# x's fourth form is spread over the first pair's products, its second form is split one product sooner, and a weight row is split ahead of h

## The chip, the cores and the metric

The kernel runs on one core of a Trainium2 chip. The metric is the device time of one execution in microseconds (us); lower is better. The engines are TensorE (PE, with PEld for its weight loads), VectorE (DVE), ScalarE (ACT), GpSimd (POOL) and SyncE (SP). SP, ACT and POOL can issue DMAs. Each engine works through its own instructions in the order in which the program wrote them, and waits for others by semaphores.

## The reference

One sequence of 512 frames with 1024 features runs through two layers. Each layer is FFN, mixer, FFN, and a gated per-layer input embedding (PLE); after each, `x = layer_norm(2 ** 0.5 * x + sublayer)`.

```python
def swiglu_ffn(x, w_gu, w_d):            # w_gu: 1024 x 5632, w_d: 2816 x 1024
    g, u = jnp.split(x @ w_gu, 2, axis=-1)
    return (jax.nn.silu(g) * u) @ w_d

for i in range(2):
    x = layer_norm(ALPHA * x + 0.5 * swiglu_ffn(x, ffn1_wgu[i], ffn1_wd[i]), ...)
    mix = mlstm_mixer(x, ...) if i == 0 else gmlp_mixer(x, ...)
    x = layer_norm(ALPHA * x + mix, ...)
    x = layer_norm(ALPHA * x + 0.5 * swiglu_ffn(x, ffn2_wgu[i], ffn2_wd[i]), ...)
    x = layer_norm(ALPHA * x + sigmoid(x @ ple_wg[i] + ple_bg[i]) * (p[i] @ ple_wp[i]), ...)
```

All of it is float32. The change touches the four FFNs and the first products of the mLSTM mixer that follows the first FFN.

## The kernel before, in words

**Numbers in two parts.** A float32 operand is split into a high part (an ACT copy to a shorter format, `hi`) and a low part (`lo = src - hi`). A product of two operands is then three matmuls (`mm3`, L394 to L398): high by high, high by low, low by high. The split of a weight tile is in `Weights.fill`: the high part on ACT at L281, the low part either on DVE (L290, or L296 when it is put off) or, for tiles in `by_dma`, by an ACT copy of the negated source (L287) and a DMA issued by POOL that accumulates the source onto it (L288).

**The queue of weights.** `Weights` holds a written-out order of tiles (`order`), each with a kind of buffer (`main`: 4 buffers, `rows`, `rowsx`, `extra`, ...). `take` hands the next split tile to a product; `release` gives a buffer back and calls `fill`, which splits the next tiles in order as long as buffers are free, the load is there, and `limit` (an index in `order`) isn't reached. While `apart` is set, low parts on DVE are not issued with the high part but put into `pending`; `lows(n)` issues the first n of them, and `take` issues those that its tile needs. While `apart` is set, `fill` also stops at a tile whose load was issued less than two products ago, as long as others are ready. When a low part is issued, its raw buffer counts as read and the next load is issued on SP.

**An FFN.** The 22 blocks of 128 hidden columns are done in chunks of 2, 4, 4, 4, 4, 4 (`FFN_CHUNKS`). The first four blocks are plain: chunk 0, and the first two of chunk 1. A plain step is one projection (`project`, gate or up, 24 matmuls of 512 columns), numbered (c, i) by chunk and step, i = 0 to 3. From then on the blocks come in pairs, and a pair's gate and up halves are computed with 7 products instead of 8 (`UpPair.product(r)`, r = 0 to 6, 24 matmuls of 256 columns each), with sums of weight blocks (`up_forms`) and sums of blocks of x (`UpForms`). The way down is done likewise for a chunk at a time, 7 group products (`Group`), which are put between the products of the next chunk: one behind each plain step, and one behind every second product of a pair. The last chunk has a plain way down (`down`), four rows of `wd` for four 128-frame blocks.

**x's forms.** `UpForms` makes four sums of blocks of x once per FFN: t1 to t4, in high and low parts. Its float32 work tiles are `x_a` (a), `x_f` twice (b and c) and `x_d` (d, for t4). The steps in `self.steps` are taken by `formed.step()` in the plain products, one each, and two each in the products (1, 2) and (1, 3): so t1 is made in (1, 1), the splits of t1 and t2 in (1, 2), and `x21` and `t4` (four DVE steps) in (1, 3). t2's split is two ACT copies and one accumulating DMA from POOL (L1047 to L1049). What is in `self.last` comes behind a product of the first pair: t3's split behind product 0, t4's high part (ACT, L1068) behind product 1, its low part (DVE, L1073) behind product 2. t4's high part goes to the tile of b, which t3's split reads; t4's low part to the tile of c. Product 2 uses t2, product 3 t1, product 4 t3, and product 6 t4.

**Behind a product of a pair** (`up_products`), in this order: the additions of the last group product to x (`group.add`), `pair.take(r)`, the group form's low part, `W.lows()`, the step of `formed.last`, `W.release()` with its splits, the silu (`pair.gate`), weight sums ahead of time (`form_ahead`); then, behind every second one, a group product, another release and a group form. `pair.take(r)` copies a PSUM bank out on ACT for r = 0, 2, 3 (L1111) and adds one on DVE for r = 1, 5 (L1114) and 4 (L1116). Products 0, 2, 4 and 6 write the same bank, products 3 and 5 another: product 4 can start when `take(2)` has read its bank.

**The last way down.** In an FFN ahead of a PLE stage, its four `wd` rows have the kinds `rowsx`, `main`, `rows`, `main`. `W.limit` stops `fill` ahead of the fourth until the products of the last chunk, and the splits of the last h, are issued.

**mLSTM's start.** `up_staged` makes the first three products of the mixer with 256 frames first, while the last blocks of x are turned (hooks), then the other 256.

Of the kernel before, what the change touches and what calls it, by code (L numbers as in the profile page):

```python
# [50 lines left out]
class Weights:  # L51
# [4 lines left out]
    def __init__(self, nc, raw_pool, split_pool):  # L56
        self.nc = nc
        self.pools, self.free = {"main": split_pool}, {"main": W_BUFS, "none": 0}
        self.raw_pools, self.raw_bufs = {"raw": raw_pool}, {"raw": RAW_BUFS}
        self.raw_free, self.raw_at, self.raw_tags = deque(range(RAW_BUFS)), {}, {}  # L60
        self.loads, self.left, self.raws = [], [], {}
        self.queues, self.held_raws = defaultdict(deque), defaultdict(deque)
        self.order, self.next_split, self.in_place, self.by_dma = [], 0, set(), set()
        self.ready, self.taken, self.held = deque(), deque(), []
        self.apart, self.pending, self.made, self.after, self.formed = False, deque(), {}, {}, set()
        self.boxes, self.rank, self.loaded_at, self.clock = [], {}, {}, 0
        self.limit, self.ahead, self.forced, self.sums = None, False, False, set()

    def open(self, kind, pool, n):
        self.pools[kind], self.free[kind] = pool, n  # L70
# [180 lines left out]
    def fill(self, most=1000, low=None, meanwhile=None):  # L251

        while most and self.next_split < len(self.order) and self.next_split != self.limit:
            kind, js, make = self.order[self.next_split]
            if not self.free.get(kind):
                return meanwhile
            for j in js or ():
                while j not in self.raws:
                    if not self.load(self.loads[j][1]):
                        return meanwhile  # L260
                if self.apart and self.ready and self.loaded_at[j] > self.clock - 2:
                    return meanwhile
            if self.ahead and not self.forced and make in self.sums and make not in self.made:
                return meanwhile
            shape = [P, 2, 512]
            if js is not None:
                while any(m not in self.formed for m in self.after.get(make, ())):
                    self.lows(1)
                src, used = self.made.pop(make, None) or make()
                shape = list(src.shape)  # L270
            hi = self.pools[kind].tile(shape, F32R, name="whi", tag="whi")
            lo = self.pools[kind].tile(shape, F32R, name="wlo", tag="wlo")
            self.free[kind] -= 1
            self.next_split += 1
            if js is None:
                make(hi, lo)
                continue
            parts = 2 if self.next_split == 1 else 1
            for i in range(parts):
                s = slice(i * shape[1] // parts, (i + 1) * shape[1] // parts)  # L280
                self.nc.scalar.activation(hi[:, s], src[:, s], AF.Copy)  # L281
                if meanwhile and make in self.in_place:
                    meanwhile()
                    meanwhile = None
                if make in self.by_dma or low == "dma" and make not in self.in_place:

                    self.nc.scalar.activation(lo[:, s], src[:, s], AF.Copy, scale=-1.0)  # L287
                    self.nc.gpsimd.dma_start(lo[:, s], src[:, s], accum_op=OP.add)  # L288
                elif not self.apart:
                    self.nc.vector.tensor_sub(lo[:, s], src[:, s], hi[:, s].bitcast(F32))  # L290
            self.ready.append((kind, (hi, lo)))
            most -= 1

            def done(make=make, used=used, src=src, hi=hi, lo=lo, late=self.apart and make not in self.by_dma):
                if late:
                    self.nc.vector.tensor_sub(lo, src, hi.bitcast(F32))  # L296
                self.formed.add(make)
                for j in used:
                    self.left[j] -= 1
                while self.load():  # L300
                    pass

            if self.apart and make not in self.by_dma:
                self.pending.append((lo, done))
            else:
                done()
        return meanwhile
# [58 lines left out]
def hybrid_trunk(ctx: ExitStack, tc, x, p, ln_g, ln_b, ffn1_wgu, ffn1_wd, ffn2_wgu, ffn2_wd,  # L366
# [125 lines left out]
    def ffn_weights(wgu, wd, name, ple=False):  # L492
        starts = [sum(FFN_CHUNKS[:c]) for c in range(LAST + 1)]

        def forms(c):
            m = FFN_CHUNKS[c] // 2

            def quarter(i, j):
                k = starts[c] + m * i
                return kp(wd)[:, k:k + m, j * 512:(j + 1) * 512]  # L500
            loads = [W.add_load(quarter(i, j), n, name) for i, j, n in ((0, 0, 2), (0, 1, 1), (1, 1, 1), (1, 0, 2))]
            return W.forms("rows", *((j, slice(None)) for j in loads))

        first = len(W.order)
        for at in range(PLAIN):
            if at == 0 or at == PLAIN - 1:
                W.add(*((kp(wgu)[:, :, c0:c0 + P], [slice(None)]) for c0 in (at * P, HID + at * P)))
            elif at % 2:
                add_pairs(wgu, at * P, HID + at * P)
        tiles = W.order[first:]  # L510
        del W.order[first:]
        for c, n in enumerate(FFN_CHUNKS):
            down_w = deque(forms(c - 1) if c else ())
            plain = plain_blocks(c)
            for i in range(2 * plain):
                W.order.append(tiles[2 * starts[c] + i])
                if down_w:
                    W.order.append(down_w.popleft())
            if plain < n:
                products = []  # L520
                for b in range(starts[c] + plain, starts[c] + n, 2):
                    products += W.up_forms(*(W.add_load(kp(wgu)[:, k:k + 4, c0:c0 + 2 * P], 1, "box")
                                             for c0 in (b * P, HID + b * P) for k in (0, 4)),
                                            by_dma=UP_BY_DMA if b == starts[c] + plain else UP_BY_DMA_2 if c < LAST else UP_BY_DMA_LAST)
                for s, product in enumerate(products):
                    W.order.append(product)
                    if down_after(c, s):
                        W.order.append(down_w.popleft())
        if ple:
            W.add_hook("rows", lambda hi, lo: turn_p.pop()(hi, lo))  # L530
        add_rows(wd, starts[LAST], 4, ["rowsx", "main", "rows", "main"] if ple else ["main", "rows", "rowsx", "rows"])
        ffn_ends.append(len(W.order) - (1 if ple else 0))


    ML_SLOTS = (2, 3, 4, 5, 6, 7, 11)
# [343 lines left out]
    def up_staged(first=False):  # L879
# [14 lines left out]
        for i, ps in enumerate(banks):  # L894
            w = W.take()
            ws.append(w)
            if i:
                up(ps, w, 0, 256, (((0,), (2, 7)) if first else ((), (0, 3)))[i - 1])
                continue
            if not first:  # L900
                run_hook()
            low_last(w, ps, 0, 256)
        low_last(ws[0], banks[0], 256, SEQ)
        for ps, w in zip(banks[1:], ws[1:]):
            up(ps, w, 256, SEQ)
        return banks

    def up_tokens(t, ws, ps, c=slice(0, 512), hook=None, release=None):
# [99 lines left out]
    class UpForms:  # L1008


        def __init__(self, pool, late):
# [33 lines left out]
            def split_t2():  # L1045
# [4 lines left out]

            self.steps = [
                x22, lambda: joined(b, 0, 1), t3, lambda: joined(c, 0, 0), lambda: vec.tensor_add(c, b, c),
                t1, split_t1, split_t2]

            d = [tmp.tile([P, 2, 256], F32, name="x_d", tag="pad", bufs=3) for _ in range(2)]

# [15 lines left out]
                for i, s in enumerate(halves):  # L1072
                    vec.tensor_sub(lo[:, s], d[i], self.t4[0][:, s].bitcast(F32))  # L1073

            self.steps += [x21, t4]
            self.last = {0: lambda: split(*self.t3, b), 1: t4_high, 2: t4_low}
            self.right = [self.quarter(0, 0), self.quarter(1, 0), self.t2, self.t1, self.t3,
                          self.quarter(1, 1), self.t4]

# [55 lines left out]
    def ffn(layer, k, rows, late, prepare=None):  # L1135
        with stage_pool("forms", 2) as fpool, stage_pool("quarters", Q_BUFS) as qpool, \
# [58 lines left out]
            for c, n in enumerate(FFN_CHUNKS):  # L1195
# [5 lines left out]
                if c == 0:  # L1201
                    formed = UpForms(tpool, late)
                W.apart, W.ahead = not plain, c > 0
                if c == LAST:
                    W.limit = ffn_ends.pop(0)
                for i in range(2 * plain):
# [16 lines left out]
                    if (c, i) in AFFINE_AT:  # L1223
                        run_affine(by_dma=True)
                    W.form_ahead(3)
                    for _ in range(1 if (c, i) < (1, 2) else 2):
                        formed.step()
                if c == 0:
                    group = Group(h, fpool, True)
                    group.form()  # L1230
                    group.form()
                else:
                    W.apart = True
                    next_group = up_products(c, n, h if c < LAST else None, plain)
                    if c < LAST:
                        next_group.form()
# [1 line left out]
                    group = next_group  # L1238
            W.limit = None
            W.fill()  # L1240
            W.apart = W.ahead = False
            return down(hs, False, norm, lazy=layer == 0, defer=prepare is not None)

    def ffn_stage(layer, k):
# [725 lines left out]
```

## Time and profile before

| what | us |
|---|---|
| median of 3 runs | 2197.59 (2197.32 to 2198.0) |
| the profiled execution | 2193.58 |
| its span, first to last instruction | 2191.9 |
| PE busy in the span | 2167.9 |
| DVE busy | 1761.8 |
| ACT busy | 1245.3 |

The mean granted clock of TensorE in the span is 0.996. A row of the timeline gives the start, the length, engine, line, operation and tiles (out<-in), and in brackets how long the engine had been idle before it and what ended that. A row of the list of waits gives who waited for whom: us in total, times, the longest. A row of the windows gives the stretch, its length, then the busy time of PE, PEld, DVE, ACT and POOL with the number of instructions, the granted clock, the DMA engines' busy share, and GB/s.

### The profile page before, as it was taken

The numbers are of one execution on the slowest core, as the hardware profiler recorded it, in microseconds if no ns is written. First come the engines' busy times: TensorE is split into PE (matmuls) and PEld (weight loads), VectorE is DVE, ScalarE is ACT, GpSimd is POOL, SyncE is SP. The second block draws the span as 40 slices with busy tenths as digits, with TensorE's granted clock in tenths as the row PEclk, the third lists the DMA queues.
The fourth block names the chain that finished last, engine by engine and source line by source line (L and its number), as shares of the span: only waits on it lengthen the run. The fifth ranks groups of instructions, "written<-read, shape, count | busy, mean of one in ns | idle before, by whom it ended". The sixth has DMA issues, their size and how long they took to land. (4 is left out here: it accounts for less than half of the span.)

```text
span 2191.9 us, 33268 instructions
## 1 busy us (share of the span) xinstructions
PE 2167.9 (99%) x13109; PEld 1934.6 (88%) x13109; DVE 1761.8 (80%) x2540; ACT 1245.3 (57%) x1712; POOL 253.8 (12%) x311
## 2 busy tenths in 40 slices
PE   9999999999999999999999999999999999999998
PEld 8899998888888889999888899998888888999987
DVE  6888887777776788888887888887788678888887
ACT  4766656464646456666445766655345455666642
POOL 1111101011101111111000111100011101111100
PEclk9999999999999999999999999999999999999999
DMA  7878764366847468787444887763338748877651
GB/s 218 195 185 192 175 166 124 78 156 134 165 112 155 124 156 206 187 202 167 144 132 131 199 194 185 177 158 125 132 77 155 163 125 202 193 189 177 137 170 58
DMA packets 232836, 346.28 MB, mean 158 GB/s; under 512 B 9780, under 2 KB 164532, under 8 KB 232680
## 3 DMA queue, kind: packets, MB, share of 16 engines
q0 software_dynamic: 56832, 117.64, 31.6%
q1 hardware_dynamic: 169232, 211.83, 29.8%
q10 hardware_dynamic: 6616, 14.69, 2.0%
q8 instruction: 103, 1.69, 0.3%
q14 instruction: 53, 0.43, 0.1%
HBM read 224.58 MB, written 2.11 MB: 103 GB/s over the span
## 5 line engine op out<-in xcount | busy, mean ns | idle before, releaser
L281 ACT ACTIVATE whi<-wbox 128x1024 fp32r<-128x1024 f32 x252 | 265.1, 1054 | 233.2 <-DVE wbox L144 99.9
L396 PE MATMUL ups<-xh,whi 128*128 128x256 f32 x1152 | 328.3, 285 | 7.8 <-ACT us L1111 7.8
L398 PE MATMUL ups<-xh,wlo 128*128 128x256 f32 x1152 | 328.1, 285 | 0.7 <-DMA wlo<-wbox 0.6
L397 PE MATMUL ups<-xl,whi 128*128 128x256 f32 x1152 | 327.9, 285 | 0.0
L396 PE MATMUL gps<-whi,fhi 128*128 128x512 f32 x644 | 253.0, 393 | 0.1
L281 ACT ACTIVATE whi<-wraw 128x1024 fp32r<-128x1024 f32 (+1 forms) x196 | 200.5, 1045 | 92.0 <-DVE wraw L121 22.6
L397 PE MATMUL gps<-wlo,fhi 128*128 128x512 f32 x644 | 252.3, 392 | 0.0
L398 PE MATMUL gps<-whi,flo 128*128 128x512 f32 x644 | 251.5, 391 | 0.0
L288 POOL DMA_DIRECT2D wlo<-wbox x160 | 135.6, 848 | 920.7 <-ACT wlo L287 502.9
L396 PEld LDWEIGHTS ups<-xh,whi 128*128 128x128 f32 x1152 | 222.8, 193 | 11.9 <-ACT us L1111 9.5
L397 PEld LDWEIGHTS ups<-xl,whi 128*128 128x128 f32 x1152 | 222.9, 194 | 2.4
L398 PEld LDWEIGHTS ups<-xh,wlo 128*128 128x128 f32 x1152 | 222.8, 193 | 1.1 <-DMA wlo<-wbox 1.1
L784 DVE TENSOR_TENSOR xt<-xt,gps 128x512 f32<-128x512 f32 x302 | 195.5, 681 | 29.1 <-PE gps L398 29.1
L290 DVE TENSOR_TENSOR wlo<-wraw,whi 128x1024 fp32r<-128x1024 f32 (+1 forms) x124 | 148.1, 1213 | 39.7 <-ACT whi L281 38.9
L281 ACT ACTIVATE whi<-wquarter 128x1024 fp32r<-128x1024 f32 (+1 forms) x140 | 135.2, 966 | 59.2 <-ACT wlo L287 20.4
L287 ACT ACTIVATE wlo<-wbox 128x1024 fp32r<-128x1024 f32 x160 | 167.1, 1044 | 0.0
L398 PEld LDWEIGHTS gps<-whi,flo 128*128 128x128 f32 x644 | 120.9, 188 | 26.9
L396 PEld LDWEIGHTS gps<-whi,fhi 128*128 128x128 f32 x644 | 121.3, 188 | 22.3 <-issue 0.2
L397 PEld LDWEIGHTS gps<-wlo,fhi 128*128 128x128 f32 x644 | 121.4, 188 | 21.3
L296 DVE TENSOR_TENSOR wlo<-wquarter,whi 128x1024 fp32r<-128x1024 f32 (+1 forms) x116 | 139.2, 1200 | 0.0
L966 DVE TENSOR_TENSOR flo<-h,fhi 128x512 fp32r<-128x512 f32 (+1 forms) x140 | 88.7, 636 | 53.5 <-ACT fhi L963 53.4
L963 ACT ACTIVATE fhi<-h 128x512 fp32r<-128x512 f32 (+1 forms) x140 | 80.3, 574 | 52.3 <-DVE h L1216 28.7
(367 smaller groups left out, 5806.8 us busy)
## 6 DMA issues: line engine op xcount, KB each, us to landing
wlo<-wbox POOLq DMA_DIRECT2D x160, 512.0 KB, 5.8
wbox<-in_ffn_wgu_dram SPq DMA_DIRECT2D x144, 512.0 KB, 4.6
wquarter<-in_ffn_wd_dram SPq DMA_DIRECT2D x64, 512.0 KB, 6.1
wraw<-in_ml_w_in_dram SPq DMA_DIRECT2D x24, 1024.0 KB, 5.8
wlo<-wraw POOLq DMA_DIRECT2D x48, 512.0 KB, 6.5
wraw<-in_gm_w_in_dram SPq DMA_DIRECT2D x15, 1024.0 KB, 5.8
wraw<-in_ffn_wgu_dram SPq DMA_DIRECT2D x17, 512.0 KB, 5.5
wraw<-in_ffn_wd_dram SPq DMA_DIRECT2D x8, 1024.0 KB, 4.9
```

Of the source, the lines that this page charges most:

```text
L281: self.nc.scalar.activation(hi[:, s], src[:, s], AF.Copy)
L287: self.nc.scalar.activation(lo[:, s], src[:, s], AF.Copy, scale=-1.0)
L288: self.nc.gpsimd.dma_start(lo[:, s], src[:, s], accum_op=OP.add)
L290: self.nc.vector.tensor_sub(lo[:, s], src[:, s], hi[:, s].bitcast(F32))
L296: self.nc.vector.tensor_sub(lo, src, hi.bitcast(F32))
L396: mm(ps, st[0], mv[0], start=start, stop=False, skip_group_check=more)
L397: mm(ps, st[0], mv[1], start=False, stop=False, skip_group_check=more)
L398: mm(ps, st[1], mv[0], start=False, stop=stop, skip_group_check=more)
L784: vec.tensor_add(dst, dst, ps)
L963: sca.activation(hi, src, AF.Copy)
L966: vec.tensor_sub(lo, src, hi.bitcast(F32))
```

## The change

- x's forms: `split_t2` is taken in (1, 1), `t1` in (1, 2), `split_t1` in (1, 3), one step per plain product. `x21` and `t4` come behind products 1 and 2 of the first pair, `t4_high` and `t4_low` behind products 3 and 4.
- The limit in an FFN ahead of a PLE stage lies behind the fourth row of `wd` instead of ahead of it.
- A new flag `hold` takes over the second meaning of `apart` (stopping at a fresh load). Behind the first FFN `apart` stays set through its way down and into `up_staged` of the mLSTM mixer, `hold` doesn't; `up_staged` issues the pending low parts one at a time between its products and then clears `apart`.

```diff
-                if self.apart and self.ready and self.loaded_at[j] > self.clock - 2:
+                if self.hold and self.ready and self.loaded_at[j] > self.clock - 2:
                     return meanwhile
...
         add_rows(wd, starts[LAST], 4, ["rowsx", "main", "rows", "main"] if ple else ["main", "rows", "rowsx", "rows"])
-        ffn_ends.append(len(W.order) - (1 if ple else 0))
+        ffn_ends.append(len(W.order))
...
             low_last(w, ps, 0, 256)
+            W.lows(1)
         low_last(ws[0], banks[0], 256, SEQ)
         for ps, w in zip(banks[1:], ws[1:]):
+            W.lows(1)
             up(ps, w, 256, SEQ)
+        W.lows()
+        W.apart = False
         return banks
...
             self.steps = [
                 x22, lambda: joined(b, 0, 1), t3, lambda: joined(c, 0, 0), lambda: vec.tensor_add(c, b, c),
-                t1, split_t1, split_t2]
+                split_t2, t1, split_t1]
...
-            self.steps += [x21, t4]
-            self.last = {0: lambda: split(*self.t3, b), 1: t4_high, 2: t4_low}
+            self.last = {0: lambda: split(*self.t3, b), 1: x21, 2: t4, 3: t4_high, 4: t4_low}
...
                 W.apart, W.ahead = not plain, c > 0
+                W.hold = W.apart
...
                     W.form_ahead(3)
-                    for _ in range(1 if (c, i) < (1, 2) else 2):
-                        formed.step()
+                    formed.step()
...
-                    W.apart = True
+                    W.apart = W.hold = True
                     next_group = up_products(c, n, h if c < LAST else None, plain)
...
             W.limit = None
             W.fill()
-            W.apart = W.ahead = False
+            W.apart, W.ahead, W.hold = (layer, k) == (0, 0), False, False
             return down(hs, False, norm, lazy=layer == 0, defer=prepare is not None)
```

More of the change, by code (lines that the diff above doesn't have):

```diff
@@ L66, in __init__ @@
         self.boxes, self.rank, self.loaded_at, self.clock = [], {}, {}, 0
-        self.limit, self.ahead, self.forced, self.sums = None, False, False, set()
+        self.hold, self.limit, self.ahead, self.forced, self.sums = False, None, False, False, set()
     def open(self, kind, pool, n):
```

## The prediction

> **What bounds the kernel now.** I read the page's first part, then TensorE's own list of waits, then windows over the places which that list names, then ACT's and DVE's timelines there.
>
> ```profile
> span 2191.9 us, 33268 instructions
> ...
> PE 2167.9 (99%) x13109; PEld 1934.6 (88%) x13109; DVE 1761.8 (80%) x2540; ACT 1245.3 (57%) x1712; POOL 253.8 (12%) x311
> ```
>
> TensorE (PE) is the bound: 2191.9 - 2167.9 = 24.0 us idle in all. No change in DVE or ACT work is worth anything by itself; only PE's waits count. The list of PE's waits:
>
> ```profile
> PE ups L396 <- ACT us L1111: 7.8, 4, 2.4
> PE dps L397 <- DVE wlo L296: 1.5, 2, 0.8
> ...
> PE sup L888 <- ACT xh L657: 1.1, 2, 0.8
> PE ups L398 <- DMA wlo<-wbox: 1.0, 2, 0.6
> PE ups L397 <- DMA t_wlo<-x_f: 0.8, 3, 0.3
> ```
>
> The first row is four waits, one in each of the four FFNs, and the last row three of the four: they lie in the first pair of up products, where x's forms are made. The second row is the last way down of the two FFNs that a PLE stage follows. The list gives waiting time only, so I measured the stretches themselves: four windows, each from the first matmul of the first pair to the first of the next pair (7 products of 24 matmuls and 3 group products of 6), then two undisturbed products, one group product, and the product behind the third FFN's long wait.
>
> ```profile
> 61.73:88.49 26.76, 25.01 (x187) 23.48 (x186) 22.72 (x34) 20.81 (x28) 5.04 (x6) 1.00 0.87 206
> 809.13:838.41 29.28, 26.54 (x187) 24.91 (x186) 23.46 (x35) 22.67 (x31) 5.09 (x6) 0.94 0.85 204
> 1212.84:1242.09 29.25, 26.53 (x187) 24.83 (x186) 23.75 (x35) 22.70 (x31) 5.10 (x6) 0.94 0.85 208
> 1833.04:1862.04 29.00, 26.54 (x188) 24.99 (x187) 23.40 (x34) 22.66 (x31) 5.09 (x6) 0.94 0.87 210
> 1212.84:1218.59 5.75, 5.75 (x49) 5.74 (x48) 5.17 (x8) 5.26 (x8) 0.85 (x1) 1.00 0.46 126
> 1218.59:1220.02 1.43, 1.43 (x9) 1.01 (x7) 1.43 (x3) 1.43 (x5) 0.86 (x1) 1.00 1.00 189
> 1230.23:1234.60 4.37, 4.37 (x25) 4.37 (x26) 2.93 (x5) 3.27 (x4) 0.84 (x1) 0.64 1.05 248
> ```
>
> Undisturbed, a product takes 5.75 / 2 = 2.875 us and a group product 1.43, so the stretch would be 7 x 2.875 + 3 x 1.43 = 24.4 us. The four are longer by 2.35, 4.87, 4.84 and 4.59: 16.65 us in all, twice the 7.8 of the list. Where the rest goes shows in the last window: after the wait, the 24 matmuls took 4.37 us at a granted clock of 0.64, 1.5 more than 2.875. The three stretches with a wait of about 2.4 us have a clock of 0.94, and the first, whose wait is shorter, 1.00. So a wait of 2.4 us here costs about 3.9.
>
> The Trainium skill, page TensorE: Matmul & The Clock Gate, sections "What's actually happening" and "Why this matters for your kernels", has the clock halved after at least one idle window of about 3.4 us, and advises against idle gaps above about 3 us. The trace differs: 2.4 us was enough.
>
> **Why PE waits there.** The third FFN, ACT first.
>
> ```profile
> 1213.33 0.42 ACT L963 ACTIVATE fhi<-h 128x256 fp32r<-128x256 f32 x1 [3.93 <-DVE h L951]
> ...
> 1216.64 1.04 ACT L281 ACTIVATE whi<-wbox 128x1024 fp32r<-128x1024 f32 x1
> 1217.59 1.04 ACT L287 ACTIVATE wlo<-wbox 128x1024 fp32r<-128x1024 f32 x1
> ...
> 1219.36 0.58 ACT L1111 ACTIVATE us<-ups 128x512 f32<-128x512 f32 x1
> ...
> 1220.79 1.04 ACT L281 ACTIVATE whi<-wbox 128x1024 fp32r<-128x1024 f32 x1
> 1221.73 1.04 ACT L287 ACTIVATE wlo<-wbox 128x1024 fp32r<-128x1024 f32 x1
> 1225.31 1.15 ACT L1068 ACTIVATE t_f<-x_d 128x512 fp32r<-128x512 f32 x2 [2.53 <-DVE xl L402]
> ...
> 1229.61 0.57 ACT L1111 ACTIVATE us<-ups 128x512 f32<-128x512 f32 x1
> ```
>
> ```profile
> 1216.52 1.29 DVE L402 TENSOR_TENSOR t<-x_a,t 128x512 fp32r<-128x512 f32 x2
> ...
> 1220.45 1.29 DVE L1021 TENSOR_TENSOR x_d<-xh,xl 128x512 f32<-128x512 f32 x2
> 1221.66 1.29 DVE L1063 TENSOR_TENSOR x_d<-x_d,x_f 128x512 f32<-128x512 f32 x2
> ...
> 1224.06 1.22 DVE L402 TENSOR_TENSOR xl<-x_f,xh 128x1024 fp32r<-128x1024 f32 x1
> ```
>
> Product 4 writes the PSUM bank that `take(2)` copies out (L1111, 1229.61 to 1230.18); PE starts it at 1230.23. The copy is in ACT's order behind `t4_high` (L1068), which sat 2.53 us because its tile replaces t3's source and so waits for t3's low part (DVE L402, 1224.06 to 1225.28). That low part is queued behind `x21` and `t4` (1220.45 to 1222.9). After its start at 1225.31, t4_high and what lies between it and the copy keep ACT busy for 1229.61 - 1225.31 = 4.3 us.
>
> **Part 1: the fourth form later.** x21 and t4 leave the last plain product; they go behind product 1's and product 2's DVE work, `t4_high` behind product 3's copy, `t4_low` behind product 4's. The work is the same (4 + 2 DVE steps of 0.6, 2 ACT steps of 0.55); only its place moves. x21 passes two residual additions, t3's low part and product 1's addition; t4 passes two more and two low parts; t4_high passes on ACT six weight splits, one silu, one h split and two bank copies. Also t1 goes from plain product 1 to 2 and its split from 2 to 3, so DVE is 1.2 us earlier from plain product 1 on (nothing stands there) and 2.4 us earlier at product 0: t3's low part ends near 1222.9.
>
> ACT gains too. Its 3.93 us wait at 1213.33 for DVE's L951 ends 1.2 us sooner (1212.1), and the 3.3 us of t1's and t2's splits that followed it are gone from there, so product 3's weights go from 1216.64 to about 1212.5, a wait for t1 on DVE (ready 1216.5) then t1's high parts, product 0's copy near 1217.2, t3's high part, product 4's weights near 1218.6, product 5's near 1220.5; the silu waits for product 1's addition (1223.5), one weight split and the h split follow, and `take(2)` runs at about 1224.9 to 1225.5. PE, without waits, ends product 3's group at 1212.84 + 4 x 2.875 + 2 x 1.43 = 1227.2. So the copy is some 1.7 us early and the wait goes, and the halved clock with it.
>
> What is late next: product 4's weights have their low part by DMA:
>
> ```profile
> wlo<-wbox POOLq DMA_DIRECT2D x1, 512.0 KB, 6.6
> ```
>
> This is the issue at 1223.07, 0.3 us after ACT's L287 of 1221.73. With that L287 near 1219.5 to 1220.5 it is issued near 1220.8 and lands near 1227.4; PE needs it at its third matmul, 1227.45. That is a tie: 0 to 0.5 us each in the three later FFNs, I take 0.25. In the first FFN, which has no affine work on DVE, all is about 1.5 us sooner. The weights behind it keep their distance to PE within some tenths, since their buffers are freed by PE's own products: 0 to 0.5 per FFN, I take 0.2.
>
> t4_low stands on DVE behind product 4's addition, which waits for product 4 itself, and product 6 waits for t4_low: three steps of 0.6 and one L296 of 1.2 are 3.0 us against product 5 and a group product, 4.3. Cover 1.3 us; if two more low parts of 1.2 come between, 1.1 us per FFN is lost.
>
> **Part 2: the second form sooner.** `split_t2` moves from plain product 2 to 1: two ACT copies and a POOL-issued accumulating DMA of the same 512 KB. On ACT it now stands ahead of a silu and a weight split (2 x 0.95 us, the silu 0.7 us later; PE runs a plain product there, 24 matmuls of which 6 take 1.43, so 5.7 us, which hides it), on POOL behind the same affine DMA as before. A plain product and a group product, 7 us, now lie between its issue and product 0: the three `t_wlo` waits go. All this is inside the 16.65.
>
> **Part 3: the fourth row.** In the two PLE FFNs the limit now takes in the fourth `wd` row. Its buffer is free by then and it shares its load with the third row, so it is split right after it.
>
> ```profile
> 1076.80 0.69 DVE L1130 SCALAR_TENSOR_TENSOR us<-us 128x512 f32<-128x512 f32 x1
> ...
> 1081.13 1.23 DVE L296 TENSOR_TENSOR wlo<-wraw,whi 128x1024 fp32r<-128x1024 f32 x1 [0.26 <-ACT whi L281]
> ```
>
> The low part at 1081.13 (it releases PE, list row 2) moves ahead of the h step at 1076.80. The raw buffer that it frees lets SP issue the next load (PLE weights) that much sooner; SP has nothing else waiting. It delays both h steps by 1.2 us, used by the third of four row products, some 2.7 us after the way down starts; that leaves tenths of cover. Gain 1.5 us for both; bounds 0 and 1.6 (two waits of the longest, 0.8).
>
> **Part 4: mLSTM's start.** Low parts there are put off behind x's last turns. PE's two waits (1.1 us) end with ACT's xh copies, and what is ahead of these on ACT stays:
>
> ```profile
> 354.98 3.89 ACT L281 ACTIVATE whi<-wraw 128x1024 fp32r<-128x1024 f32 x4
> ```
>
> So no gain. The weight loads that wait for the put-off low parts start later, by the turns and products that these parts now stand behind, and the next splits on DVE's list do too. I take 0; bounds -1 and +1.1, the size of the two waits.
>
> **Sum.** 16.65 + 1.5 = 18.15, less 3 x 0.25 + 4 x 0.2 = 1.55: 16.6 us. The profiled execution took 2193.58 us (span 2191.9), so 2177.0 for such a one; the median is 2197.59, and 16.6 off that is 2181.0.
>
> **Rivals.**
> A. The low parts by DMA set the pace: if ACT does not get product 4's weights done sooner, they land at 1229.6 as now, PE waits 2.2 us and the clock halves (1.5): 3.7 of 4.8 stays in three FFNs, the gain is 16.6 - 11 = 5.6, time 2192. Without the halving 2.2 stays: gain 10, 2187.6. For it: the landing ties with the need. Against: only ACT's order held that split back. Chance 0.12.
> B. DVE gives it back later. In the stretches DVE is busy 23.4 to 23.75 of 29 us; in 24.4 us that is 97%. PE's pause was when DVE caught up, and the following pairs run with DVE behind. If 2 us per FFN come back: gain 8.6, 2189. Against: DVE starts the stretch 2.4 us ahead and does no more than before. Chance 0.10.
> C. Slower: product 4's accumulating DMA stretches, as reads, loads and accumulation now crowd into 24 us (DMA share 0.85 in 29). Beyond 6.6 us each us is paid in three FFNs, and from 2.4 us on the clock adds 1.5. To lose the 16.6 and 4.4 more takes 7 us in each: a landing of 12 us, giving 2202. Chance 0.05.
> D. The halved clock does not come from these waits and stays: gain 16.6 - 3 x 1.5 = 12.1, 2185.5. For it: three cases only. Against: all three lie right behind the waits. Chance 0.08. The rule of the Trainium skill quoted above (TensorE: Matmul & The Clock Gate) would have it so, since 2.4 us is less than its idle window.
> E. The fourth row is still held back (a new `hold` test) or not freed: 2182.5. Chance 0.03.
>
> **How the numbers follow.** Forecast 0.62. 0.2% (4.4 us) is about what a measurement of this kernel can tell from no change. A to B contain 0.03 that stay within it; C is 0.05 slower; the rest is faster, 0.92. The range: all of 18.15 and mLSTM's 1.1 us gained gives 2178.3, and I go to 2177.5, since list row 2's price leaves out PE's slow restart; upward to B and the lighter A, 2189.5.
>
> **What would show it.** Right: no `ups <- us L1111` wait above 0.3 us; the four stretches at 24.4 to 25.4 us with clock 1.00; no `t_wlo` wait; L296 ahead of the first h step and no `dps` wait; the two `sup <- xh` waits unchanged. Wrong: a wait on `wlo<-wbox` of over 1 us at product 4 (A), DVE without idle and new `ups` waits on L296 or on `t_f` (B), a clock under 1.00 in a stretch without a wait (D).

## The result, and the profile after

The changed kernel takes 2179.46 us (median of 5 runs, 2178.20 to 2180.83), the kernel before in the same session 2197.59 us (median of 5 runs, 2196.14 to 2198.00): a ratio of 0.9918, 95% interval 0.9903 to 0.9932. That is 18.1 us less (14.9 to 21.3 by the interval); the forecast was 2181.0. The profiled execution of the changed kernel took 2179.46 us, with a span of 2177.8, so between the two profiled executions the difference is 2191.9 - 2177.8 = 14.1 us. The two differences are taken apart below.

First part of the page of the changed kernel:

```profile
span 2177.8 us, 33285 instructions
...
PE 2161.0 (99%) x13109; PEld 1931.7 (89%) x13109; DVE 1761.4 (81%) x2540; ACT 1244.9 (57%) x1712; POOL 253.8 (12%) x311
```

DVE, ACT and POOL did the same work as before to within 0.4 us. PE is 6.9 us less busy with as many matmuls (a matmul at the halved clock counts as longer), and idle for 2177.8 - 2161.0 = 16.8 us instead of 24.0. So half of the 14.1 us is idle time. Of the 6.9, the three stretches of 3.41 us at half the clock in the profile of before explain 5.1 at most; the rest lies beside the waits, where matmuls of 0.28 to 0.39 us no longer start 0.12 apart and so overlap less. In the first FFN's stretch, whose clock was 1.00, PE was busy 25.01 us before and 24.24 now.

PE's waits in the changed kernel:

```profile
PE ups L398 <- DMA wlo<-wbox: 4.3, 4, 1.7
PE warm L1926 <- POOL ident masks.py:199: 1.4, 1, 1.4
PE sup L888 <- ACT xh L657: 1.1, 2, 0.8
PE xps L649 <- DVE xt L764: 0.8, 2, 0.4
```

Three rows of before are gone: the copy of the bank (7.8 us), the fourth row's low part (1.5) and t2's low part (0.8). mLSTM's two waits are the same, 1.1. One row grew: the wait for low parts that come by DMA, from 1.0 to 4.3.

The four stretches, from the first matmul of the first pair to the first of the next pair. Columns as in the prediction: length, then busy time of PE, PEld, DVE, ACT and POOL, granted clock, DMA share, GB/s.

```profile
62.20:86.44 24.24, 24.24 (x188) 23.45 (x186) 20.73 (x32) 18.01 (x25) 4.18 (x5) 1.00 0.89 221
807.18:832.37 25.19, 24.49 (x187) 23.50 (x186) 22.13 (x33) 18.36 (x26) 4.24 (x5) 1.00 0.93 226
1205.62:1231.54 25.92, 24.52 (x188) 23.53 (x187) 22.20 (x33) 18.42 (x26) 4.25 (x5) 1.00 0.92 223
1822.14:1848.29 26.15, 24.49 (x188) 23.51 (x186) 22.72 (x34) 18.95 (x26) 4.25 (x5) 1.00 0.93 229
```

The clock is 1.00 in all four. They are shorter by 2.52, 4.09, 3.33 and 2.85 us, 12.8 in all. The first is without any wait, so 24.24 is the undisturbed length (the prediction's 24.4 took 1.43 us for a group product, which is 1.34 to 1.40 here). The three others are over it by 0.95, 1.68 and 1.91, and the third FFN shows where. PE and ACT:

```profile
1219.95 0.28 PE L397 MATMUL ups<-xl,whi 128*128 128x256 f32 x1
1221.64 0.39 PE L398 MATMUL ups<-xh,wlo 128*128 128x256 f32 x1 [1.41 <-DMA wlo<-wbox]
```

```profile
1212.33 1.05 ACT L287 ACTIVATE wlo<-wbox 128x1024 fp32r<-128x1024 f32 x1
...
1217.64 0.57 ACT L1114 ACTIVATE us<-ups 128x512 f32<-128x512 f32 x1
```

The copy of `take(2)` (L1111 before, L1114 now) ends at 1218.21, 1.6 us ahead of product 4's first matmul (1219.84). But the third matmul of product 4 needs the low part of its weights. Their L287 came in good time, POOL issued the DMA at 1213.66, and it landed only 7.9 us later, at 1221.6:

```profile
wlo<-wbox POOLq DMA_DIRECT2D x1, 512.0 KB, 7.9
```

DVE, the engine of rival B, shows the opposite of a bottleneck: it stood idle and waited for product 4.

```profile
1224.63 0.69 DVE L1119 TENSOR_TENSOR us<-us,ups 128x512 f32<-128x512 f32 x1 [2.65 <-PE ups L398]
```

At the last way down ahead of the first PLE stage, DVE now makes the low parts of the third and of the fourth row in one go (x2) ahead of the first h step (L1133):

```profile
1069.61 2.35 DVE L296 TENSOR_TENSOR wlo<-wraw,whi 128x1024 fp32r<-128x1024 f32 x2
1071.88 0.69 DVE L1133 SCALAR_TENSOR_TENSOR us<-us 128x512 f32<-128x512 f32 x1
```

### The profile page after: what moved, and what is told of

The parts are those of the page before. It is cut to its first block, busy times and chain, and to the rows that moved or that the text cites. A ratio compares the mean times of both kernels' runs of the same rounds, so it can differ in the third digit from the quotient of the medians.

```text
span 2177.8 us, 33285 instructions
## 1 busy us (share of the span) xinstructions
PE 2161.0 (99%) x13109; PEld 1931.7 (89%) x13109; DVE 1761.4 (81%) x2540; ACT 1244.9 (57%) x1712; POOL 253.8 (12%) x311
## 5 line engine op out<-in xcount | busy, mean ns | idle before, releaser
L290 DVE TENSOR_TENSOR wlo<-wraw,whi 128x1024 fp32r<-128x1024 f32 (+1 forms) x120 | 143.5, 1213 | 38.1 <-ACT whi L281 37.2
L287 ACT ACTIVATE wlo<-wbox 128x1024 fp32r<-128x1024 f32 x160 | 167.1, 1044 | 0.0
L397 PEld LDWEIGHTS gps<-wlo,fhi 128*128 128x128 f32 x644 | 121.4, 188 | 21.3
```

The lines of the kernel that those rows point to most:

```text
L397: mm(ps, st[0], mv[1], start=False, stop=False, skip_group_check=more)
```

## The experiments

All kernels do the same arithmetic; only the place or the engine of some steps differs. The median of the kernel before beside them was 2196.39, 2196.34 and 2197.02 us in three sessions, from 27, 21 and 7 runs between 2194.06 and 2199.32.

**Parts 1 and 2 alone.** On the kernel before:

```diff
-                t1, split_t1, split_t2]
+                split_t2, t1, split_t1]
-            self.steps += [x21, t4]
-            self.last = {0: lambda: split(*self.t3, b), 1: t4_high, 2: t4_low}
+            self.last = {0: lambda: split(*self.t3, b), 1: x21, 2: t4, 3: t4_high, 4: t4_low}
-                    for _ in range(1 if (c, i) < (1, 2) else 2):
-                        formed.step()
+                    formed.step()
```

> Parts 1 and 2 alone: x's forms as in the changed kernel; the fourth row's limit and mLSTM's start as before. My theory (the parts lie at different waits and add): the whole gain but part 3's, so 1.5 to 2.1 us slower than the changed kernel, near 2181.3; the four stretches from the first pair's start to the next pair's at 24.2, 25.2, 25.9, 26.1 us as in the changed kernel; the two dps waits on L296 of 0.8 us there as before. Rival (the parts hide one another): the gain is far from the whole less 2.

2181.94 us, ratio 0.9935 (0.9922 to 0.9947): 14.5 us. The stretches are 24.24, 25.27, 25.29 and 26.87, and the two waits for the fourth row's low part stay. So nearly all of the gain is in these two parts. The wait of the second FFN was at product 6 in this execution, the others at product 4.

**Part 3 alone, and part 4 alone.**

```diff
-        ffn_ends.append(len(W.order) - (1 if ple else 0))
+        ffn_ends.append(len(W.order))
```

> Part 3 alone: the limit behind the fourth row. My theory: the two dps waits on L296 go, and with PE's slow restart behind them the time falls by 1.5 to 2.1 us, to about 2195.6. Rival: the h steps, 1.2 us later, hold the third row product, and the gain is under 0.5.

2193.57 us, ratio 0.9992 (0.9984 to 1.0001), which is 1.8 us with an interval of -0.2 to 3.5. Both waits of 0.76 are gone from PE's list. The sum of 1.5 agrees with it, though the time alone can't tell it from nothing.

Part 4 is `hold` and the `lows` calls of the diff, without parts 1 to 3.

> Part 4 alone: apart kept through the first FFN's way down and up_staged. My theory: PE waits for ACT's xh copies behind four weight splits of 3.9 us on ACT, which stay; 0 within 0.5 us, and the two sup waits on xh stay at 0.2 and 0.8. Rival: the four low parts on DVE (4.6 us) held the turns; then both waits go and it is 1.1 to 1.5 us faster.

2196.63 us, ratio 1.0002 (0.9993 to 1.0011): nothing. The waits of 0.24 and 0.84 stay.

**The kernel before again.** No edit, for a second profiled execution.

> The kernel before, once more, for the span and clock of each timed execution. The profiled gain is 14.1 us of span, the gain of the medians 18.1. My theory: time less span is the same 1.7 us in every execution, and the executions differ in span and granted clock, since a wait of 2.4 us halves the clock for one or for more windows of 3.4 us according to where it falls in them: spans from 2191.9 to about 2196 with clocks down from 0.996. Rival: the spans are all 2191.9 and the 4 us are outside of the span.

2195.30 us median, ratio 0.9999 (0.9991 to 1.0008); the profiled execution took 2197.11, span 2195.4, 3.5 more than the first profiled one. Its stretches are 26.59, 31.98, 29.48 and 29.17, together 117.22 against 114.29 us: 2.9 of the 3.5. In the second FFN there were two waits, 2.43 us on the copy and 2.25 us on a low part by DMA of product 6, and the halved clock came behind the second. So the kernel before has landings and halvings that differ from one execution to the next, and the profile that the prediction was made on was one of its better executions: its 2193.58 us lie below all of the 55 that were run beside the experiments. The expectation was right that time less span stays at 1.7 to 1.8 us and that the spans differ (2192.8 to 2197.9), but not that the clock sets them: the median of the 55 is 2196.5 us at a mean clock of 0.996 and 2196.0 at 0.998.

**Part 1 without part 2.** The fourth form later, but t1 and t2 where they were.

```diff
-            self.steps += [x21, t4]
-            self.last = {0: lambda: split(*self.t3, b), 1: t4_high, 2: t4_low}
+            self.last = {0: lambda: split(*self.t3, b), 1: x21, 2: t4, 3: t4_high, 4: t4_low}
-                    for _ in range(1 if (c, i) < (1, 2) else 2):
+                    for _ in range(2 if (c, i) == (1, 2) else 1):
```

> Part 1 without part 2: x21, t4 and t4's split behind products 1 to 4, but t1 and t2 are made and split in (1, 1) and (1, 2) as before; fourth row and mLSTM as before. My theory: the wait on take(2) goes, but ACT does t1's and t2's splits where it did, so product 4's low part by DMA is issued only about x0 + 10.2 us and lands at + 16.8 as before, while PE needs it at + 14.5: waits on wlo<-wbox of about 2.3 us at product 4 in the three later FFNs take the place of the waits on the copy, the t_wlo waits of 0.25 stay; stretches near 27 us, gain 5 to 8 us. Rival (the whole loss was t4_high ahead of the copy, and where t1 and t2 are split is worth only the t_wlo waits): stretches at 24.7 to 25.2, gain 12 to 13.

2196.16 us, ratio 0.9997 (0.9988 to 1.0006): nothing, and the gain that was expected fell. The waits on the copy are gone, and PE's list shows what took their place:

```profile
PE ups L398 <- DMA wlo<-wbox: 12.6, 7, 2.9
PE dps L397 <- DVE wlo L296: 1.5, 2, 0.8
```

At product 4 this is rival A as it was described: waits of 2.03, 1.77 and 2.63 us in the three later FFNs, where 2.3 were expected. Product 5's low part was late as well, which the expectation had left out: 2.87, 0.70 and 2.35 us in the first three FFNs, with a halved clock behind the first and the last of these. On ACT, t1's and t2's splits still stand behind the wait for DVE's h, in front of the weight splits (third FFN; the stretch begins at 1215.09):

```profile
1215.58 0.42 ACT L963 ACTIVATE fhi<-h 128x256 fp32r<-128x256 f32 x1 [3.93 <-DVE h L951]
1216.00 1.15 ACT L401 ACTIVATE t<-x_a 128x512 fp32r<-128x512 f32 x2
1217.06 1.05 ACT L1047 ACTIVATE t_wlo<-x_f 128x1024 fp32r<-128x1024 f32 x1
1218.01 1.04 ACT L1049 ACTIVATE t_whi<-x_f 128x1024 fp32r<-128x1024 f32 x1
...
1224.05 1.05 ACT L287 ACTIVATE wlo<-wbox 128x1024 fp32r<-128x1024 f32 x1
```

Product 4's L287 stands 9.0 us into the stretch (1224.05), against 6.7 in the changed kernel (1212.33 - 1205.62). The waits of 1.77 and 2.35 us are those of this FFN.

**Part 2 without part 1.**

```diff
-                t1, split_t1, split_t2]
+                split_t2, t1, split_t1]
-                    for _ in range(1 if (c, i) < (1, 2) else 2):
+                    for _ in range(3 if (c, i) == (1, 3) else 1):
```

> Part 2 without part 1: t2 split in (1, 1), t1 in (1, 2) and (1, 3), but x21 and t4 in (1, 3) and t4's split behind products 1 and 2 as before. My theory: t3's low part on DVE ends where it did, so t4_high and the copy behind it come where they did; the t_wlo waits go, but PE then waits that much longer for the copy: stretches as before within 0.5 us, gain 0 to 1.5. Rival (the second form's place makes the gain): most of the 14 us.

2195.46 us, ratio 0.9996 (0.9987 to 1.0005): nothing. The `t_wlo` waits are gone, and the waits on the copy are longer:

```profile
PE ups L396 <- ACT us L1111: 10.2, 4, 3.3
```

So each of the two parts is worth nothing alone, and both together 14.5 us: the copy and the low parts of product 4's and 5's weights were two limits at the same place, and each hid the other.

**Which DMA sets what is left?** In the first pair of the changed kernel two of the seven low parts come from DVE, the five others by DMA. Two kernels give one of the five to DVE:

```diff
-    by_dma=UP_BY_DMA if b == starts[c] + plain else ...
+    by_dma=UP_BY_DMA_2 if c == 1 else UP_BY_DMA if b == starts[c] + plain else ...
```

> The changed kernel, with the low part of product 4's weights of the first pair (chunk 1) on DVE and not by DMA. My theory (what is late next is that DMA, with three other transfers in flight): the waits on wlo<-wbox at product 4 go, DVE has 2.65 us idle there to take the 1.2; stretches of 24.2 to 24.6 us in the four FFNs, 3.5 to 4.5 us less than the changed kernel, near 2175.5. Rival (DVE is the next bound): new ups waits on L296 or L402 of 1 us and more, no gain.

Product 4's by DVE: 2177.92 us, ratio 0.9916 (0.9903 to 0.9930), 1.5 below the changed kernel where 3.5 to 4.5 were expected. Product 4 waits no more, but product 6 does, for its own low part by DMA: 1.64, 1.20 and 0.28 us. The stretches are 24.24, 26.12, 25.69 and 24.77.

> The changed kernel, with the low part of product 5's weights on DVE, product 4's by DMA as it is. My theory (product 4's landing, 7.2 to 8.2 us, is stretched by product 5's DMA issued 1.9 us behind it): it lands after about 6.6 us again, the waits at product 4 fall from 0.7, 1.4 and 1.7 to 0 to 0.5, and 2 to 4 us are gained on the changed kernel. Rival (the two loads of wbox and wquarter stretch it): the landing stays near 7.9, and so do the waits.

Product 5's by DVE instead (`by_dma=(1, 3, 4, 6)`): 2181.61 us (2180.12 to 2186.95), ratio 0.9937 (0.9925 to 0.9949), not the 2 to 4 us of gain that were expected. Product 4 still waits 1.07, 0.57 and 1.90 us, the last with a halved clock behind it. Its low part landed after 7.3, 7.1 and 8.4 us in the three later FFNs, and not after 6.6. So product 5's transfer is not what stretches product 4's, or not by enough to show in one profiled execution.

**Both, product 4's and product 6's, on DVE** (`by_dma=(1, 3, 5)` for c == 1):

> The changed kernel with the low parts of the first pair's product 4 and of the product after next both made by DVE (two steps of 1.2 us more) instead of an accumulating DMA. What sets the pace of the first pair now? Theory 1, the DMAs: product 4's was late by 0.7 to 1.7 us, with it gone the next one was late by 0.3 to 1.6; with both gone the stretches come to 24.4 to 24.8 us, no wait on wlo<-wbox is left there, and the kernel is 1.5 to 2.5 us shorter than with the first alone: 2175.5 to 2176.5. Theory 2, DVE (rival B of the prediction): it is busy 22.2 us of the stretch now, 24.6 with both steps, as much as PE's 24.4, so PE gets waits on DVE's L296 of 0.5 to 1.5 us in each of three FFNs and the kernel takes 2178 to 2181.

2173.83 us (2173.64 to 2174.20), ratio 0.9895 (0.9880 to 0.9909). This beats both kernels, by 5.6 us the changed one. Its four stretches:

```profile
62.25:86.49 24.24, 24.24 (x188) 23.46 (x186) 23.38 (x34) 17.04 (x24) 2.51 (x3) 1.00 0.75 196
807.13:831.37 24.24, 24.24 (x187) 23.45 (x186) 24.17 (x35) 16.46 (x24) 2.54 (x3) 1.00 0.84 225
1204.67:1228.91 24.24, 24.24 (x188) 23.46 (x187) 24.17 (x35) 16.45 (x24) 2.58 (x3) 1.00 0.85 226
1819.53:1843.77 24.24, 24.24 (x188) 23.46 (x187) 24.17 (x35) 16.45 (x24) 2.56 (x3) 1.00 0.84 225
```

All four are undisturbed. DVE (third busy figure) is at 24.17 of 24.24 us and yet PE waits nowhere in them: DVE's order has enough lead that it is never the last. The working of the expectation was too careful: what the kernel with product 4's alone has over the undisturbed length, 1.88 + 1.45 + 0.53 = 3.9 us, is all gained, not half of it. And in span it is 2177.8 - 2172.4 = 5.4 us below the changed kernel, which had 0.95 + 1.68 + 1.91 = 4.5 in its stretches and another wait of 0.53 in the next pair. So all that was left over in the FFNs were these DMAs.

**mLSTM's start.** `take` gets an argument that sets `limit` for one call, and `up_staged` uses it in mLSTM for its third product, so that one weight tile is split ahead of x's last two half turns and three behind them:

```diff
-            w = W.take()
+            w = W.take(1 if one and i == 2 else None)
```

> The changed kernel with one more edit, at mLSTM's start: ahead of x's last two half turns ACT splits one weight tile instead of four (1 x L281 of 0.97 us in place of 3.89), and the three others behind the turns. DVE's order stays as it is. My theory (part 4 gave nothing because ACT's four splits, not DVE's low parts, hold the two xh copies that PE waits for): the copies come 2.9 us sooner, both sup <- xh waits (0.24 and 0.84) go, the start-to-start excess of 1.4 us at them with them, the span is about 1.1 to 1.4 us shorter than the changed kernel's, 2178.1 for its median of 2179.46; no sup <- whi wait of over 0.3 comes in their place. Rival (the last turns are bound by PE's transposes or by DVE's xl behind the copies): a wait on xl or on whi takes their place and nothing is gained.

2178.11 us, ratio 0.9914 (0.9897 to 0.9931), span 2176.1. ACT's order there:

```profile
352.93 1.04 ACT L281 ACTIVATE whi<-wraw 128x1024 fp32r<-128x1024 f32 x1
355.12 1.51 ACT L656 ACTIVATE xf<-xps,cols 128x128 f32<-128x128 f32 x4 [1.15 <-PE xps L651]
356.66 0.64 ACT L659 ACTIVATE xh<-xf 128x512 fp32r<-128x512 f32 x1
```

```profile
PE ups L400 <- DMA wlo<-wbox: 3.9, 5, 1.4
PE warm L1928 <- POOL ident masks.py:199: 1.4, 1, 1.4
PE xps L651 <- DVE xt L766: 0.8, 2, 0.4
```

The `sup <- xh` row is gone and nothing took its place. The two waits were held by ACT's splits, as part 4's working had it. The trace shows them gone; the 1.4 us between the medians lie within the runs' own scatter.

**That and product 4's low part on DVE together:**

> Both gains together: the changed kernel with product 4's low part on DVE and with the one split ahead of mLSTM's last turns. Theory: the two are far apart in time and add up, 1.3 + 1.2 us below the changed kernel's 2179.46, so 2176.5 to 2177.5, ratio to the kernel before 0.9905 to 0.991. Rival: what one saves is waited for in the next FFN's DMAs, and the time is that of the first alone, 2178.

2177.03 us (2175.95 to 2177.37), ratio 0.9908 (0.9893 to 0.9923), inside the range for adding up, but only 0.9 below the one alone, which is less than either scatters: which of the two holds stays open. Product 6 waited 1.90 us in the third FFN.

**The changed kernel again:**

> The changed kernel again, unaltered, for another profiled execution. If the landing of product 4's low part is set by what is in flight beside it (the two weight loads and product 5's transfer, the same in each execution), the waits at product 4 come again at 0.7, 1.4 and 1.7 us within 0.3, and the landings at 7.2, 7.9 and 8.2. If it varies by itself, they move by over 0.5 us each and their sum of 3.8 by over 1. Time 2178 to 2181 either way.

2179.19 us, ratio 0.9920 (0.9905 to 0.9934), profiled span 2178.5. Product 4's low part landed after 6.3, 6.3 and 8.4 us in the three later FFNs instead of 7.2, 7.9 and 8.2, here in the third FFN:

```profile
wlo<-wbox POOLq DMA_DIRECT2D x1, 512.0 KB, 6.3
```

There was no wait at product 4 in the second and third FFN, and one of 1.89 us in the fourth, with a halved clock behind it. Low parts of product 5, of product 6 and of the next pair were late by 0.2 to 0.5 us in four places instead. The landing is not fixed by the transfers that the program issues beside it; of the two theories the second holds. In the second and third FFN POOL issued the DMA 1.2 us behind SP's load of the next box, where it had been 0.9 and 0.55 before; whether that decides was not tried.

## Why the prediction was right, and which terms were off

**The bound and the cause were right.** With the copy's wait gone in four places, and ACT's and DVE's total work the same, the four stretches lost 12.8 us and had no halved clock in the first profiled execution of the changed kernel (the second had one, behind a low part by DMA). The prediction laid all of a stretch's excess to that wait and the clock behind it, which is too much for the first FFN: of its 1.75 us of idle time before, 0.79 were the copy's, and 0.64 and 0.32 were low parts by DMA at products 5 and 6, the 1.0 of the list. They went too. The forecast of ACT's order held: product 4's DMA was forecast for 1220.8, 7.95 us into the stretch, and POOL issued it 8.04 into it; the copy at 1224.9 to 1225.5, 12.1 to 12.7 in, and it came at 12.0.

**Part 1, the term that was mis-sized: the tie at product 4.** The step "lands near 1227.4 [...] That is a tie: 0 to 0.5 us each" used one landing time of the trace of before, 6.6 us (product 4's took 6.3 to 6.8 in its four FFNs). It took 7.2, 7.9 and 8.2 in the three later FFNs, and product 4 waited 0.70, 1.41 and 1.66 instead of 0.25 each. With the 0.53 in the next pair, 4.3 us were left where 3 x 0.25 + 4 x 0.2 = 1.55 were taken, 2.75 more. The sum of 16.6 is 2.5 above the 14.1 between the profiled executions, so this term is about all of the difference. The DMA engines' share was 0.77 over the 6.6 us of the transfer that was used (1223.07 to 1229.67 before) and 0.95 over the 7.9 us of the same transfer now (1213.66 to 1221.60); the duration from the emptier stretch was taken over as one figure without a spread. The share alone does not set it: in the changed kernel's second profile the same transfer took 6.3 us at a share of 1.04, so what stretches it stays open. Two of the four stretches (25.92 and 26.15) came out above the 24.4 to 25.4 that were named as the sign of being right.

**From the profile to the median.** 18.1 us between the medians is more than the 14.1, because the kernel before's usual executions are longer than its profiled one: 2197.11 in the second profiled one, of which 2.9 us were found in the same four stretches. That the forecast of 2181.0 is so near 2179.46 has a part of luck in it: the low parts by DMA were under-priced by 2.75, while an ordinary execution of before had 4.0 more to lose (2197.59 - 2193.58) than the one that was worked from.

**Part 2** was priced at nothing of its own ("All this is inside the 16.65"), and rightly so in the sum. But part 1 without it gains nothing either. The working had the reason, that the 3.3 us of t1's and t2's splits go from ahead of product 3's and 4's weights on ACT; the expectation of 5 to 8 us for part 1 alone used it for product 4, but left product 5 and the halved clock out.

**Parts 3 and 4** went as worked out: 1.5 against two waits gone and 1.8 (-0.2 to 3.5) measured; 0 against 0.

**The rivals.** A named the right next limit, and its sign, over 1 us on `wlo<-wbox` at product 4, came in two FFNs (1.41 and 1.66). But its cause did not: ACT had product 4's weights done in time, and only with part 2 taken out did it hold them back. What came is C's mechanism at a small size: the transfer stretched beyond 6.6 us, to 8.2 in the first profile and 8.4 in the second, and PE paid for it; C's slower kernel, with a landing of 12, fell. So A's sign could not tell the two apart. B fell: DVE can be at 24.17 of 24.24 us without costing PE anything. E fell. D needs a paragraph.

**The halved clock.** The prediction took 1.5 us behind each wait of 2.4, and left it open whether shorter or longer ones do it. Within a profiled execution, the halved stretches begin whole multiples of 3.413 us apart: in the first profile of before at 827.22, 1229.99 and 1851.22, with 402.77 and 621.23 us between them, 118.0 and 182.0 times 3.413. So time is cut into windows that do not start with the wait. With the windows laid out like this, all fourteen profiles agree (the kernel's two ends left out): PE was idle for 1.88 to 2.97 us in each of the 15 windows behind which the clock went to half, and for 1.70 at most in every other but one, which had 1.87. Part 3 alone shows both outcomes in one execution, here in pairs of such windows (length, PE busy first, granted clock third from the end):

```profile
825.90:829.31 3.41, 1.92 (x16) 1.92 (x17) 2.42 (x5) 3.41 (x7) 0.75 (x1) 1.00 1.07 299
829.31:832.72 3.41, 2.90 (x25) 2.70 (x24) 2.83 (x4) 3.41 (x5) 0.86 (x1) 1.00 1.06 257
1228.67:1232.08 3.41, 0.97 (x9) 0.94 (x8) 1.44 (x3) 3.41 (x7) 0.85 (x1) 1.00 1.05 297
1232.08:1235.49 3.41, 3.41 (x19) 3.41 (x17) 1.99 (x4) 2.34 (x3) 0.84 (x1) 0.50 1.04 229
```

The waits are nearly the same, 2.40 and 2.44 us. The first lies across a border, 1.5 us of it in one window, and the clock stays; the second lies within one window, and the next 3.41 us run at half the clock (in one of the 15 cases, with PE still waiting at first, it was two windows, 6.83 us). The Trainium skill, page TensorE: Matmul & The Clock Gate, section "What's actually happening", has the window free-running and 3413 ns long. These traces agree. The Trainium skill also has the clock halved after at least one idle window; here about 1.9 us of idle time in a window was enough. So rival D fell, since the halving does come from these waits; but the prediction's price was too regular, since a wait of 2.4 us brings the halving only where enough of it falls within one window. Of the 27 waits of 1.9 to 3.3 us in all profiles, 15 were followed by it. By these counts a wait of 2.4 costs, as an estimate, 2.4 + 1.5 x 15 / 27 = 3.2 on average and not 3.9, and which of them pay changes from one execution to the next.

## What to carry to other kernels

When a wait is removed, price the next-latest operand of the same instruction with a spread of durations from busy stretches, not with the one row at hand: here the next one, a DMA of 512 KB, took 6.3 to 9.0 us for products 4 and 5 of the changed kernel. Two edits that are worth nothing each can be worth 14 us together when they lift two limits at the same place, so a test of "one part alone" can't be read as that part's share. And an engine that is 99.7% busy over a stretch is not yet the limit: look for its waits on others and for those who wait on it. Where there are none that matter, it can be the best place for work that a DMA does late.

## What the hardware did that was not expected

- In all fourteen profiles the clock was halved by the idle time within a fixed window of 3.413 us, from about 1.9 us on, and not by the length of a wait: 2.89 us across a border left it at 1.00, 1.89 within one window halved it for 3.41 us.
- The same accumulating DMA of 512 KB from POOL, issued in the same place of the program, landed after 7.9 us in one execution and 6.3 in another (third FFN). With t1's and t2's splits left in place (part 1 alone), one with little else in flight landed after 4.5 us, and one with two loads and two more such DMAs around it after 10.3.
